# Weight loads in whole thirds, and the last half's routing with other squares, integer indices and other filler products, in a one-layer encoder with a mixture of experts

## The chip, the core and the metric

The kernel runs on one core of a Trainium2 chip. The metric is device time in microseconds (us), the median of several executions. A time with a profile is told apart from it: the profiler's execution has a span of its own (first to last instruction of the program) and a time of its own.

Engines in the rows below: PE is TensorE (PEld its weight loads), DVE VectorE, ACT ScalarE, POOL GpSimd, SP SyncE. A q behind the name (SPq) means the engine's sequencer, which issues DMAs. L599 is line 599 of the kernel.

## The reference

One encoder layer over x of 1024 tokens x 1024 features in float32: an attention branch and a gated short convolution, both projected and added to x, and then a hierarchical mixture of experts, which the change is about:

```python
h2 = rmsnorm(x, norm2_g)
g_logits = h2 @ w_rg + b_rg                      # 4 groups
grp = argmax(g_logits)                           # the best group of each token
e_in = (h2 @ w_re + b_re).reshape(t, 4, 8)[grp]  # the 8 experts of that group
top_p, top_i = top_k(softmax(e_in), 2)           # the best two of them
gates = softmax(g_logits)[grp] * top_p / sum(top_p)
out[t] = x[t] + sum over both: gate * (silu(h2 @ w_gate[e]) * (h2 @ w_up[e])) @ w_down[e]
```

There are 32 experts with an inner width of 256. The weights of one expert are 3 MB: gate and up for the first and the second half of the features, and down, three thirds of 1 MB.

## The kernel before

**Stages.** Projections and attention, then the merge of both branches in two halves of 512 tokens. For each half `out_half` computes x after the first residual, in eight column blocks of 128 (`mm`), transposes each to token rows (`turn`), writes the rows to the output and, times the norm's gain, to a table in DRAM (`h2n`), and multiplies them with the router's weights. `route` then makes the lists of the half. The routing of the first half runs beside the second half's merge; **the routing of the second half stands alone** between the merge and the experts (about 643 to 663 us of the profile).

**The last half's routing.** In `turn(7)` TensorE transposes block 7 into PSUM, ScalarE copies the block to SBUF (L850), VectorE multiplies it with the gain (L851), and `square` (L842) has ScalarE square the copied rows with a sum per token. VectorE adds the sums (L887), POOL raises the mean to the power -0.5 (L82), and VectorE scales the logits (L893). A chain of small VectorE operations follows: maximum and index per token (L904, L905), a cast of the index to float (L907), the one-hot of the group, the same for the expert (L918, L919, cast L921), and the one-hot of both experts, `ob` (L928). TensorE turns `ob` into positions (`pos`, L932 to L935), VectorE builds the matrix `A` from them (L945), and TensorE multiplies the token numbers with `A` to get the list of tokens of each expert (L952). POOL gathers the rows of experts 0 and 1 from `h2n` by that list (L1121), and TensorE transposes the gathered rows (L1132).

**Products that compute nothing.** To keep TensorE running in this stretch, `busy` (L898) issues 7 products (14 instructions) on the logits and 6 (12 instructions) on the masked expert logits, and 18 products of 512 columns follow the count (L962). Their results are not read. TensorE runs its instructions in the order in which they stand in its queue.

**The experts.** For each expert TensorE transposes the gathered rows (`px`), multiplies them with gate and up (`pgu`), ScalarE takes the silu (L1151), VectorE the product (L1153), and after two transposes (`ph`) TensorE multiplies with down (`py`). ScalarE scales the result into a buffer (L1170), and POOL adds it to the output's rows by an indirect DMA (L1173). The products run on two parts of each operand: every half third of the weights is converted to a high part (ScalarE, L1107) and a low part (VectorE, L1108), six halves for one expert. The order of ScalarE's and VectorE's work in this stage is written out by hand; `used()` says when the next half is converted.

**The stream of weights.** `load(p, s)` brings half `s` of third `p` (L599). The first 18 thirds come whole (`WHOLE`), into 16 places (12 and 13 in two halves each); places 2 and 0 are used again by thirds 16 and 17. From third 18 on every half is a DMA of its own of 512 KB into a ring of 31 half slots: those of all places except 5, whose halves hold the experts' results, and one extra tile, `more`. A load waits until its slot's last content is converted, and by a dependency written into the code for the landing of the load `DEPTH` = 4 halves before:

```python
h = 2 * p + s - DEPTH
self.tc.add_manual_dep(ins.ins, self.loads[h // 2, h % 2].ins.name, dep, reason="depth")
```

All loads go through SP's queue; half 1 of third 18 goes through POOL's, behind the two first gathers. `behind(a, b)` puts instruction a after b in the planner's order, without a wait where both are on one engine. Outside of the stage with the order by hand, a planner sets the order of each engine's queue from the dependencies and its own estimates.

## Time and profile before

| | before |
|---|---|
| median of 3 runs | 977.77 us (977.6 to 978.74) |
| the profiled execution, its own time | 980.05 us |
| its span | 977.8 us |
| PE busy / DVE / ACT / POOL | 949.3 / 736.3 / 582.7 / 115.2 us |
| mean granted clock of TensorE | 0.988 |
| DMA | 188.76 MB in 82749 packets |

The profiled execution took somewhat longer than the runs without a profile. The granted clock is a share of 2.4 GHz: 1.00 is 2.4 GHz, 0.50 is 1.2 GHz, and a value between is a stretch with both. "DMA share" is the mean busy share of the core's 16 DMA engines. The span has one stage in which TensorE, ScalarE, VectorE and the DMAs are all at work: the experts, from about 663 us to 963 us.

### The profile page before, as it was taken

Reading aid. Unit: us, or ns where it says so; the run is one execution under the profiler, and the core shown is the slowest. Engines: PE = TensorE matmul, PEld = TensorE weight load, DVE = VectorE, ACT = ScalarE, POOL = GpSimd, SP = SyncE. Lnnn points to the kernel's source line nnn. Section 1 sums busy time; section 2 is a strip of 40 time slices with the busy share of each in tenths; the row PEclk is TensorE's granted clock in tenths of the full one; section 3 lists DMA queues with packets and bytes.
Section 4 is the critical chain, followed back from the end, with each engine's and each line's share of the span. In section 5 each row is a group of like instructions: output and inputs, shape, how many; then the busy total and the mean of one; then the engine's idle time right before and its main releaser. Section 6 shows DMA issues by size and latency. Waiting matters only on the chain. (4 is left out here: it accounts for less than half of the span.)

```text
span 977.8 us, 13838 instructions
## 1 busy us (share of the span) xinstructions
PE 949.3 (97%) x4649; PEld 750.3 (77%) x4649; DVE 736.3 (75%) x1407; ACT 582.7 (60%) x1039; POOL 115.2 (12%) x90
## 2 busy tenths in 40 slices
PE   8999999999999999999999999979999999999993
PEld 5888888888878888888888888856777777777662
DVE  5777777878779656568765786478999999999882
ACT  4644555555544433346344435447999999899872
POOL 2222000000000000000000000013333232232211
PEclk9999999999999999999999999989999999999997
DMA  7201101000114233317677988768999999999993
GB/s 252 91 12 60 41 30 33 33 23 22 34 57 170 80 118 109 119 44 234 198 258 240 345 302 307 233 218 255 330 346 340 338 335 352 342 326 341 329 355 68
DMA packets 82749, 188.76 MB, mean 193 GB/s; under 512 B 10924, under 2 KB 28076, under 8 KB 80628
## 3 DMA queue, kind: packets, MB, share of 16 engines
q1 hardware_dynamic: 54772, 153.93, 45.3%
q0 software_dynamic: 7312, 17.60, 8.0%
q10 hardware_dynamic: 20592, 16.32, 5.0%
q8 instruction: 37, 0.61, 0.3%
q14 instruction: 36, 0.29, 0.1%
HBM read 166.55 MB, written 29.36 MB: 200 GB/s over the span
## 5 line engine op out<-in xcount | busy, mean ns | idle before, releaser
L1108 DVE TENSOR_TENSOR wh<-we,wh 128x1024 fp32r<-128x1024 f32 x186 | 219.8, 1217 | 29.7 <-ACT wh L1107 29.7
L1107 ACT ACTIVATE wh<-we 128x1024 fp32r<-128x1024 f32 x186 | 189.4, 1056 | 15.3 <-DMA we<-we 7.7
L70 PE MATMUL pgu<-wh,xT 128*96 128x512 f32 x768 | 190.5, 396 | 0.2 <-ACT xT L59 0.2
L70 PEld LDWEIGHTS pgu<-wh,xT 128*96 128x96 f32 x768 | 121.3, 161 | 49.9 <-ACT xT L59 0.4
L70 PE MATMUL py<-wh,hT 128*96 128x512 f32 x384 | 95.3, 395 | 3.8 <-DVE hT L60 2.0
L70 PEld LDWEIGHTS py<-wh,hT 128*96 128x96 f32 x384 | 61.4, 161 | 32.7 <-DVE hT L60 3.4
L70 PE MATMUL pc<-hT,wc_0s 128*128 128x512 f32 x288 | 77.5, 397 | 0.0
L70 PE MATMUL pc<-hT,wc_1s 128*128 128x512 f32 x288 | 75.8, 396 | 0.0
L1173 POOL DMA_INDIRECT out<-we,idx x32 | 52.6, 1644 | 183.0 <-ACT we L1170 127.4
L82 POOL TENSOR_TENSOR rstd_x<-ms_x,mhalf 128x1 f32<-128x1 f32 (+1 forms) x10 | 6.5, 651 | 573.7 <-DMA h2n<-rows 453.1
L70 PE MATMUL pq<-wq,hT 128*128 128x512 f32 (+1 forms) x384 | 71.2, 342 | 0.9 <-POOL wq L60 0.6
L70 PEld LDWEIGHTS pq<-wq,hT 128*128 128x128 f32 x384 | 59.5, 190 | 10.2 <-ACT hT L59 1.1
L70 PEld LDWEIGHTS pc<-hT,wc_1s 128*128 128x128 f32 x288 | 52.5, 188 | 9.3
L59 ACT ACTIVATE pT<-pp 128x512 fp32r<-128x512 f32 x44 | 26.1, 595 | 55.7 <-PE pp L425 55.7
L70 PEld LDWEIGHTS pc<-hT,wc_0s 128*128 128x128 f32 x288 | 52.1, 188 | 8.8 <-DVE wc_0s L60 0.3
L70 PE MATMUL po<-M,wo_1s 128*128 128x512 f32 x192 | 46.7, 391 | 0.0
L70 PE MATMUL po<-M,wo_0s 128*128 128x512 f32 x192 | 46.2, 390 | 0.0
L410 ACT ACTIVATE s<-s,nm 128x384 f32<-128x384 f32 (+1 forms) x64 | 36.9, 578 | 12.4 <-DVE nm L404 8.2
L70 PEld LDWEIGHTS po<-M,wo_1s 128*128 128x128 f32 x192 | 36.0, 188 | 8.8 <-DVE M L60 0.4
L70 PEld LDWEIGHTS po<-M,wo_0s 128*128 128x128 f32 x192 | 36.0, 188 | 7.5
L1121 POOL DMA_INDIRECT xg<-h2n,idx x32 | 35.9, 1122 | 47.7 <-PE px L1132 34.1
L1170 ACT ACTIVATE we<-py,gr 96x512 f32<-96x512 f32 x64 | 39.9, 672 | 2.4 <-PE py L70 2.4
(430 smaller groups left out, 1747.6 us busy)
## 6 DMA issues: line engine op xcount, KB each, us to landing
we<-we SPq DMA_DIRECT2D x153, 512.0 KB, 7.3
we<-we SPq DMA_DIRECT2D x16, 1024.0 KB, 7.0
sgl<-sgd SPq DMA_DIRECT2D x32, 256.0 KB, 3.6
x<-x SPq DMA_DIRECT2D x8, 512.0 KB, 4.2
wg_0r<-wcol SPq DMA_DIRECT2D x16, 256.0 KB, 2.8
wg_1r<-wcol SPq DMA_DIRECT2D x16, 256.0 KB, 2.7
wo_0r<-wo SPq DMA_DIRECT2D x16, 256.0 KB, 3.3
wo_1r<-wo SPq DMA_DIRECT2D x16, 256.0 KB, 3.6
```

What stands on the lines that cost most here:

```text
L59: a = self.nc.scalar.activation(hi, src, AF.Copy)
L70: return self.nc.tensor.matmul(*a, **k, skip_group_check=onto)
L82: self.powed = nc.gpsimd.tensor_tensor(out=r, in0=ms, in1=self.mhalf[:, :n], op=ALU.pow)
L410: ex = nc.scalar.activation(s[:, i, :nk], s[:, i, :nk], AF.Exp, bias=nm[:, i:i + 1], accum_out=sm[:, i:i + 1])
L1107: a = self.nc.scalar.activation(hl[:, 0], src, AF.Copy)
L1108: v = eng.tensor_tensor(out=hl[:, 1], in0=src, in1=hl[:, 0].bitcast(F32), op=ALU.subtract)
L1121: return self.nc.gpsimd.indirect_dma_start(out=xg[:CAP], out_offset=None, in_=self.h2n, in_offset=off, bounds_check=S, oob_is_err=False)
L1170: nc.scalar.activation(y[:C, c * 512:(c + 1) * 512], pys[c][:C], AF.Copy, scale=gate)
L1173: nc.gpsimd.indirect_dma_start(out=T["out"], out_offset=off, in_=y[:C], in_offset=None, bounds_check=S - 1, oob_is_err=False, compute_op=A ...
```

## The change

Two parts. **Stream:** thirds from 18 on come whole too, 1 MB in one DMA, except in places 12 and 13, which still take halves. The ring is the list `PLACES` of 15 places; the tile `more` is gone. A load waits for the landing of the load three thirds before. Third 18 goes whole through POOL's queue. **Routing of the last half:** block 7 is squared from PSUM, and its copy to SBUF comes behind the squares; its product with the gain is put behind the mean, and that of block 6 behind the low part of block 7; the casts L907 and L921 are gone and the integer indices are operands themselves; the `busy` products and the 18 at L962 are replaced by `fill`, products of two constants with 256 columns: 5 before block 7's transposes, 4 after its router product, 22 after the logits' transposes, 8 after the positions and 20 after the count. The position and list products are put behind the fills that stand before them.

```diff
...
 LATE = (60, 94, 94)
-WHOLE = 18
-DEPTH = 4
+DEPTH = 3
+PLACES = (2, 0, 1, 3, 4, 6, 7, 8, 9, 10, 11, 12, 13, 14, 15)
 TAP = 512
...
             r = rhs[k // 4][:, k % 4]
-            self.mm3(out, hl[:, 0, sl], hl[:, 1, sl], r[:, 0, :], r[:, 1, :], k == 0, k == n - 1)
+            last = self.mm3(out, hl[:, 0, sl], hl[:, 1, sl], r[:, 0, :], r[:, 1, :], k == 0, k == n - 1)
             if k == n // 2 - 1 and mid is not None:
                 mid()
+        return last
...
-        whole = p not in (12, 13) and p < WHOLE
+        whole = self.place(p) not in (12, 13)
         if (p, s) in self.loads:
...
         elif p >= 16 and whole:
-            self.raw[p] = self.raw[(2, 0)[p - 16]]
+            self.raw[p] = self.raw[self.place(p)]
         j = self.order[p]
         to, sl = (self.raw[p], slice(0, 2048)) if whole else (self.half_of(p, s), slice(s * 1024, (s + 1) * 1024))
-        q = self.nc.gpsimd if (p, s) == (18, 1) else self.nc.sync
+        q = self.nc.gpsimd if p == 18 else self.nc.sync
         ins = q.dma_start(to, self.T["we"][j // 3, j % 3, :, sl])
...
             self.behind(ins, self.wrote)
-        if (p, s) == (18, 1):
+        if p == 18:
             self.behind(ins, self.gathered)
...
             dep = mybir.DependencyInfo(mybir.DependencyClass.Sync, mybir.DependencyReason.DATA)
-            h = 2 * p + s - DEPTH
-            self.tc.add_manual_dep(ins.ins, self.loads[h // 2, h % 2].ins.name, dep, reason="depth")
+            self.tc.add_manual_dep(ins.ins, self.loads[p - DEPTH, s].ins.name, dep, reason="depth")
+
+    def place(self, p):
+
+        return p if p < 16 else PLACES[(p - 16) % len(PLACES)]
...
+        p = self.place(p)
         if p in (12, 13):
             return self.raw[p, s]
-        if p < 16:
-            return self.raw[p][:, s * 1024:(s + 1) * 1024]
-        return self.slots[(2 * p + s - 32) % len(self.slots)]
+        return self.raw[p][:, s * 1024:(s + 1) * 1024]
...
             po = ps.tile([P, 512], F32, name=f"po_{half}_{i}", tag=("pg", "pp")[i % 2], bufs=2)
-            self.proj(po, wg, half, rhs=self.M, mid=(lambda: turn(i - 1)) if i > 0 else None)
+            self.proved = self.proj(po, wg, half, rhs=self.M, mid=(lambda: turn(i - 1)) if i > 0 else None)
             self.added = nc.vector.tensor_add(x2, po, x2)
             self.x2s = [self.sgp.tile([P, 512], F32R, name=f"x2s_{half}_{i}_{b}", tag="sg", bufs=2) for b in range(2)]
-            self.split(x2, *self.x2s)
-
-        def square(i):
+            self.xlow = self.split(x2, *self.x2s)[1]
+            if i == 7 and half == 1:
+                self.fill(5, self.proved, None)
+
+        def square(i, pt=None):
             for t in range(4):
-                if i < 6:
+                if pt is not None:
+                    sq, R = self.sq[:, t % 2 * P:(t % 2 + 1) * P], pt[:, t]
+                elif i < 6:
                     sq, R = self.sq[:, 0:2 * P].rearrange("p (b c) -> p b c", b=2), self.rows[:, :, 0, t]
...
             R, hg = self.rows[:, i % 2, 0], self.rows[:, i % 2, 1]
-            nc.scalar.activation(R, pt, AF.Copy)
+            fast = i == 7 and half == 1
+            if fast:
+                square(7, pt)
+            copied = nc.scalar.activation(R, pt, AF.Copy)
+            if fast:
+                self.behind(copied, self.squared)
+                self.squared = copied
             self.gained.append(nc.vector.tensor_tensor(out=hg, in0=pt, op=ALU.mult,
...
             for b in range(2):
-                nc.tensor.matmul(pl, self.wrt[:, i].rearrange("p a c -> p (a c)"), self.x2s[b],
-                                 start=(i == 0 and b == 0), stop=(i == 7 and b == 1))
-            if i % 2 == 1 or i == 6:
+                m = nc.tensor.matmul(pl, self.wrt[:, i].rearrange("p a c -> p (a c)"), self.x2s[b],
+                                     start=(i == 0 and b == 0), stop=(i == 7 and b == 1))
+            if fast:
+                self.fill(4, m, None)
+            elif i % 2 == 1 or i == 6:
                 square(i)
...
         for i in range(8):
+            if i == 7:
+                self.idle = ps.tile([P, 512], F32, name=f"idle_{half}", tag="pg", bufs=2)
             mm(i)
...
         for t in range(4):
-            nc.tensor.matmul(plt[:, t], lT[:, t * P:(t + 1) * P], self.twice[:2 * NW], start=True, stop=True)
+            m = nc.tensor.matmul(plt[:, t], lT[:, t * P:(t + 1) * P], self.twice[:2 * NW], start=True, stop=True)
+        if half == 1:
+            m = self.fill(22, m, None)
         s1 = new([4], "s1")
...
         r = self.rstd(rp, s1, 4, D, "x2")
+        if half == 1:
+            self.behind(self.gained[7], self.meant)
         if half == 1:
...
-        def busy(x, n):
-            for i in range(n if half == 1 else 0):
-                nc.tensor.matmul(self.pl[:, 0:x.shape[1]], self.ident[:, 0:2 * NW], x, start=True, stop=True)
-
-        busy(lt.rearrange("p t c -> p (t c)"), 7)
         gl, el = lt[:, :, 0:NG], lt[:, :, 8:8 + NE].rearrange("p t (g j) -> p t g j", g=NG)
...
             nc.vector.max_index(gi[:, t], gm[:, t], lt[:, t, 0:8])
-        gf = new([4], "gf")
-        nc.vector.tensor_copy(gf, gi[:, :, 0])
+        gf = gi[:, :, 0]
         og = new([4, NG], "og")
...
         nc.vector.tensor_tensor(out=es, in0=el, in1=bc(og[:, :, :, None], [P, 4, NG, NJ]), op=ALU.mult)
-        busy(work[:, 256:384], 6)
         ei = new([4, NJ], "ei")
...
         ec = new([4, 2], "ec")
-        nc.vector.tensor_copy(ec, ii[:, :, 0:2])
-        nc.vector.scalar_tensor_tensor(ec, bc(gf[:, :, None], [P, 4, 2]), float(NJ), ec, op0=ALU.mult, op1=ALU.add)
+        nc.vector.scalar_tensor_tensor(ec, bc(gf[:, :, None], [P, 4, 2]), float(NJ), ii[:, :, 0:2], op0=ALU.mult,
+                                       op1=ALU.add)
         O = self.O[:, :, ts, :]
...
         pf = pp.rearrange("p t e -> p (t e)")
-        nc.tensor.matmul(pf, self.uob[:, 0, :], ob.rearrange("p t e -> p (t e)"), start=True, stop=False)
+        first = nc.tensor.matmul(pf, self.uob[:, 0, :], ob.rearrange("p t e -> p (t e)"), start=True, stop=False)
+        if half == 1:
+            self.behind(first, m)
         for t in range(3):
             nc.tensor.matmul(pp[:, t + 1:4], self.uob[:, 1, :], bc(ob[:, t:t + 1], [P, 3 - t, NE]), start=False, stop=False)
-        nc.tensor.matmul(pp, self.uob[:, 1, :], bc(self.osum[:, None, :], [P, 4, NE]), start=False, stop=True)
+        m = nc.tensor.matmul(pp, self.uob[:, 1, :], bc(self.osum[:, None, :], [P, 4, NE]), start=False, stop=True)
+        if half == 1:
+            m = self.fill(8, m, None)
         bi = new([4, 4, NE], "bg", F32R)[:, 0:2]
...
             for t in range(4):
-                nc.tensor.matmul(pI, A[:, c, t], bi[:, c, t], start=(c + t == 0), stop=(c + t == 4))
+                x = nc.tensor.matmul(pI, A[:, c, t], bi[:, c, t], start=(c + t == 0), stop=(c + t == 4))
+                if half == 1 and c + t == 0:
+                    self.behind(x, m)
         if half == 0:
...
             counted = nc.tensor.matmul(pn, self.uob[:, 1, :], self.osum, start=True, stop=True)
-            for i in range(18):
-                warm = nc.tensor.matmul(self.pl, self.uob[:, 1, 0:2 * NW],
-                                      self.O.rearrange("p a t e -> p (a t e)"), start=True, stop=True)
-                self.behind(warm, counted)
+            self.fill(20, counted, None)
             mx = new([1], "mx")
...
+    def fill(self, n, at, to):
+
+        for i in range(n):
+            m = self.nc.tensor.matmul(self.idle[:, 0:2 * P], self.uob[:, 1, :], self.uob.rearrange("p a b -> p (a b)"),
+                                      start=True, stop=True)
+            self.behind(m, at)
+            at = m
+        return at
+
     def half(self, p, s):
...
             self.behind(self.added, v)
-            self.behind(self.gained[6], self.added)
+            self.behind(self.gained[6], self.xlow)
...
         run = [self.expert(e, lambda c, s, e=e: self.w[3 * e + c, s], self.used, xgs[e % 2], xts[e % 2],
-                           lambda e=e: self.slots[0] if e == NE - 1 else self.half_of(5, e % 2),
+                           lambda e=e: self.half_of(2, 0) if e == NE - 1 else self.half_of(5, e % 2),
                            self.idx[:CAP, 1, e:e + 1], self.gr[:CAP, 0, e:e + 1], self.gr[:CAP, 1, e:e + 1])
...
             self.gathered = self.gather(xgs[e], self.idx0[:CAP, e:e + 1])
-        order = [(p, s) for p in [2, 0, 1] + list(range(3, 16)) for s in range(2)]
-        self.slots = [self.half_of(*h) for h in order if h[0] != 5]
-        self.slots.insert(4, self.sp6.tile([P, 1024], F32, name="more"))
         for p in range(17, 19):
...
```

## Rows read from the trace of the kernel before

**Rows 1.** Busy time by stretch: us, busy (instructions) by engine, clock, DMA share, GB/s
```profile
692.00:907.00 215.00, 215.00 (x1083) 155.01 (x1082) 198.23 (x235) 199.82 (x281) 65.13 (x48) 1.00 1.03 341
907.00:957.00 50.00, 47.10 (x226) 32.41 (x225) 40.66 (x48) 40.12 (x58) 10.83 (x7) 1.00 1.00 335
```
**Rows 2.** ScalarE in order of time: start, us, instruction [idle before <-releaser]
```profile
898.03 0.47 ACT L1151 ACTIVATE sg<-pgu,gr 96x256 f32<-96x256 f32 x1 [0.35 <-PE pgu L70]
...
907.20 0.47 ACT L1151 ACTIVATE sg<-pgu,gr 96x256 f32<-96x256 f32 x1 [0.34 <-PE pgu L70]
...
909.44 1.06 ACT L1107 ACTIVATE wh<-we 128x1024 fp32r<-128x1024 f32 x1 [0.82 <-DMA we<-we]
...
949.25 0.48 ACT L1151 ACTIVATE sg<-pgu,gr 96x256 f32<-96x256 f32 x1
...
956.61 0.47 ACT L1151 ACTIVATE sg<-pgu,gr 96x256 f32<-96x256 f32 x1 [0.56 <-PE pgu L70]
```
**Rows 3.** Waits from 860 to 966 us: who for whom, total, times, longest
```profile
ACT wh L1107 <- DMA we<-we: 7.7, 7, 1.9
```
**Rows 4.** TensorE in order of time, one expert's transposes
```profile
683.33 0.82 PE L1132 MATMUL px<-ident,xg 96*128 96x96 f32 x8
```
**Rows 5.** DMA queues, 692 to 907 us: packets, MB, share of 16 engines
```profile
q1 hardware_dynamic: 16763, 61.03, 78.5%
q0 software_dynamic: 5244, 12.12, 24.3%
```
**Rows 6.** Instructions of L1107 by stretch: us, busy (count), clock, DMA share, GB/s
```profile
692.00:907.00 215.00, 141.22 (x140) 1.00 1.03 341
```
**Rows 7.** All engines in order of time, the last half's routing
```profile
643.54 0.60 ACT L850 ACTIVATE rows<-pt 128x512 f32<-128x512 f32 x1 [0.43 <-PE pt L848]
...
644.17 0.31 ACT L842 ACTIVATE sq<-rows 128x128 bf16<-128x128 f32 x1
...
644.99 0.68 DVE L851 TENSOR_TENSOR rows<-pt,g 128x512 f32<-128x512 f32 x1
...
645.13 1.08 PE L885 MATMUL plt<-twice,work 80*128 80x40 f32 x8 [0.78 <-DVE work L882]
...
649.21 0.17 DVE L907 CAST gf<-gi 128x4 f32<-128x4 uint32 x1
...
651.95 2.36 PE L898 MATMUL pl<-work,ident 128*80 128x128 f32 x12
652.38 0.22 DVE L928 TENSOR_TENSOR ob<-O 128x128 bf16<-128x128 bf16 x1
...
654.15 0.22 PE L932 MATMUL pos<-ob,uob 128*128 128x128 bf16 x1
...
654.56 0.48 DVE L940 TENSOR_TENSOR work<-O,pos 128x128 f32<-128x128 bf16 x2 [1.63 <-PE pos L935]
...
657.58 5.54 PE L962 MATMUL pl<-O,uob 128*80 128x512 bf16 x18
...
662.84 0.76 PEld L1132 LDWEIGHTS px<-ident,xg 96*128 96x128 f32 x8 [0.19 <-DMA xg<-h2n,idx]
```
**Rows 8.** PE by stretch: us, busy (count), granted clock, DMA share, GB/s
```profile
646.00:648.00 2.00, 0.21 (x2) 0.73 0.98 377
...
652.00:654.00 2.00, 2.00 (x12) 0.56 1.05 430
...
656.00:658.00 2.00, 1.33 (x10) 0.79 0.03 8
658.00:660.00 2.00, 2.00 (x6) 0.50 0.00 0
660.00:662.00 2.00, 2.00 (x9) 0.85 0.79 209
```
**Rows 9.** DMA queues, 692 to 697 us, halves of weights alone: all packets
```profile
DMA packets 543, 1.97 MB, mean 393 GB/s; under 512 B 63, under 2 KB 63, under 8 KB 543
```
**Rows 10.** DMA queues, 651 to 655 us, whole thirds of weights alone: all packets
```profile
DMA packets 223, 1.68 MB, mean 420 GB/s; under 512 B 18, under 2 KB 18, under 8 KB 18
```

## The prediction

> **What bounds the kernel now.** I read the busy shares by stretch first. From 692 to 907 us TensorE has work in every microsecond, and the DMA engines are as full, while VectorE and ScalarE keep some 7% free [rows 1]. So in the long stretch of the experts two resources are at their limit at once, and the question is which of them ends an expert. ScalarE's order of time tells it. The silu of one expert (L1151) follows that of the one before by 9.17 us, from 898.03 to 907.20, and waits for TensorE's product [rows 2]: up to there TensorE sets the pace. From 909.44 on the conversions of the weights (L1107) wait for DMA [rows 2]. The table of waits has seven such waits, 7.7 us in all [rows 3].
>
> What that costs is read from the silus. Between 907.20 and 949.25 lie four experts and 42.05 us, where 4 x 9.17 makes 36.68: 5.4 us too many. The next interval is 7.36 us where 8.35 were due, as the last expert has no successor whose eight transposes (0.82 us [rows 4]) come in between; so 1.0 comes back. **4.4 us are lost to late weights**, all of it after 907.
>
> Why weights come late is a matter of counting. In the 215 us from 692 to 907 the queue of the weights moved 61.03 MB [rows 5], 116.4 halves of 524,288 bytes, and ScalarE converted 140 [rows 6]. The ring of buffers gave up 23.6 halves of lead and was empty two microseconds later, when the first wait comes. In the 45 us that are left, to the last conversions at about 952 on an undisturbed pace, another 45 x 23.6/215 = 4.9 halves are missing. They cost 4.4 us, 0.90 us each.
>
> The second place is the last half's routing, 643 to 663 us: a chain of small VectorE operations with two visits to TensorE, which ends when the first gathered rows arrive and the transposes of expert 0 begin, at 662.84 [rows 7]. Nothing hides it. What delays expert 0 delays all 32, as TensorE is full afterwards.
>
> **The routing, step by step.** *Squares from PSUM.* Now the copy L850 starts at 643.54 and the squares at 644.17 [rows 7]. Reading the transposes in place, the squares start where the copy does: 0.63 us gained. They are the same four instructions; that PSUM is slower to read than SBUF is not seen (the copy takes 0.60 for 512 columns). The copy then runs beside the mean and the power that follow, and so does the product with the gain (two of L851 at 0.68 each, of which the change ties the last behind the mean [rows 7]); without that cover it would cost its 0.68 in front of the logits. Its write to h2n leaves SP some 0.7 us later, and so do the loads queued behind it on SP, the last ones to be converted of all that is loaded by then. The product of column block 6 ends later too, and ScalarE's queue, which issues its write, must wait for it. If the planner puts that issue in front of the squares they lose the 0.63 again; I take 0, as nothing early reads that write.
>
> *Two casts fall away*, L907 and its like L921: 2 x 0.17 = 0.34 us of a VectorE chain without gaps [rows 7]. The operations that now read integers have the same shapes; a slower reading of integers is bounded by the casts themselves, so 0 to 0.34, and I take 0.34.
>
> *TensorE's dummy products.* Today 12 products of L898 run from 651.95 for 2.36 us. The one-hot sum `ob` is ready at 652.38 + 0.22 = 652.60, but the position product L932 stands behind them and starts at 654.15, and VectorE sits idle for 1.63 us before L940 [rows 7]. The new fills hang on no data of the chain: 22 go off after the logits' transposes (L885, over at 646.21), 8 after the positions, 20 after the counts. What a fill lasts is bounded by L962, 18 products of 512 columns in 5.54 us [rows 7], of which some 3.1 are at half clock [rows 8]: (3.1 + 2 x 2.4)/18 = 0.44 us for one at half clock, 0.22 for 256 columns. So 22 take at most 4.8 us and are over at about 651.1, just before `ob`, now due at 651.6. The 1.55 us between 652.60 and 654.15 shrink to a hand-over of some 0.15: 1.40 gained. Against that, TensorE may have been idle before the positions and run them at 1.2 GHz. From 654.15 to 654.56 their chain takes 0.41 us; doubled, it costs up to 0.4. I take 0.3. Sum: 0.63 + 0.34 + 1.40 - 0.3 = **2.1 us**, between 1.0 (squares and casts bring nothing, positions at half clock) and 2.4.
>
> **The stream.** Whole thirds instead of halves, three in flight instead of four halves, 15 places instead of 31 half slots; places 12 and 13 still take halves. What one byte costs is read from stretches in which one kind runs alone: halves (4 KB packets) 393 GB/s [rows 9], whole thirds (8 KB packets) 420 GB/s [rows 10]. So 512 KB takes 1.334 or 1.248 us, and with 13 of 15 places whole a half saves 0.0745. In the experts' stretch the weights' queue holds 78.5% of the engines' time [rows 5], 215 x 0.785/116.4 = 1.450 us per half; less the saving, 1.3755. If gathers and scatters (24.3%) keep their time, 215 us bring 122.7 halves, and the deficit falls from 23.6 to 17.3.
>
> The lead shrinks too. The ring has 30 halves for 31; a place is free only when both its halves are converted, and a half is usable only when its whole has landed: half a unit to one each. I take 2.5, so 21.1 are left of 23.6. From 692 to 952 the deficit eats 260 x 17.3/215 = 20.9 of them: just enough. That is too close to call free, and I leave one half missing, 0.9 us. Of 4.4 us **3.5 come back**. With no saving at all 260 x 23.6/215 = 28.5 are wanted and 7.4 missing: 6.7 us lost, 2.3 more than today. With half the saving (119.5) 3.7 are missing, 3.3 us, a gain of 1.1. The deeper queue gives nothing by itself, as the engines are full [rows 1].
>
> The Trainium skill (DMA: Bandwidth & Descriptors, Measured) sets 1 MiB as the size from which a DMA reaches at least 75% of the peak, and lets far more be expected of the doubled size; by it no half would be missing and the sum would be 2.1 + 4.4 = 6.5 us. Rows 9 and 10 speak against so large a step: with several loads in flight the two sizes differ by 6.9%.
>
> Whole load 18 goes through POOL's queue and now waits for both halves of place 1. Behind it stands the gather for expert 2, which cannot start before expert 0's transposes anyway: 0.
>
> **Sum.** 2.1 + 3.5 = 5.6 us. The profiled execution took 980.05 us (span 977.8), 2.3 over the median of 977.77. Against its own time that is 974.4; carried to the median, **972.2 us**.
>
> **Rivals.** *A, the forecast:* both parts work, 970 to 974. Chance 0.47.
>
> *B, a cold start.* The last fills are 20 x 256 columns where 18 x 512 stand now, which kept TensorE busy until the gather came. At half clock 20 last 4.4 us, at full clock half of that, and up to 2 us more are then empty before the transposes. What an empty TensorE brings here stands in rows 8: the clock falls within 646 to 648, with 0.21 of 2 us busy, and again within 656 to 658, and each time stays at 1.2 GHz under full load for a while, some 6.8 and 3.4 us by the shares. If the experts start so, half of that is lost, 1.7 to 3.4: 973.9 to 975.6. For it: nothing fills the gap. Against: the fills may end late enough. Chance 0.24. The Trainium skill (TensorE: Matmul & The Clock Gate, The HAM clock gate) has it that the slow state is the default and activity releases it; rows 8 agree.
>
> *C, the saving is lost in the mix:* beside gathers and scatters a longer packet may be stalled in proportion. Half or none of the saving: 974.6 to 978.0. Against: rows 5 give the weights 61.03 MB at 78.5%, 362 GB/s of engine time, not far under the 393 of rows 9, so most of a packet's time is the same as alone. Chance 0.19.
>
> *D, slower:* the weights' stream gets slower, because scatters stall longer packets for longer and loads land in lumps of 1 MB. The place is the ring after 900 us. At an unchanged rate the ring's loss (2.3) outweighs the routing's gain (2.1); each 1% below that loses 1.2 of 116.4 halves, 1.4 over 260 us, 1.3 us. At 2% less the time is 980.6. Against: rows 10. Chance 0.07.
>
> *E, the change doesn't do what it says:* the planner sets ScalarE's write in front of the squares, or a fill in front of the positions. 0.6 to 1.4 us less gained: 972.8 to 973.6. Chance 0.03.
>
> **How the numbers follow.** A measurement of this kernel tells 0.2%, 2 us, from no change. Faster by more: A, B but for 0.04 at its far end, the upper half of C, E: 0.81. Within: 0.12, from the ends of B and C. Slower: 0.07, D. The range runs from 970.0 (all of 4.4 and 2.4 back is 971.0, and 1 us for what the median may hold beyond the profiled run) to 977.0, which leaves out D and the end of C.
>
> **What would show it.** The waits of L1107 for DMA should nearly vanish, the silus keep 9.17 us to the end, the weights' queue carry more than 61.03 MB in 215 us. The positions should follow `ob` within 0.2 us and expert 0's transposes start near 660.8. I am wrong if waits for DMA stay or start before 900, or if the granted clock is 0.5 while the first products of the experts run.

## The result and the profile after

The changed kernel takes **983.67 us** (median of 6 runs, 981.13 to 988.56) against 977.89 for the kernel before (6 runs beside it): ratio 1.006, 95% interval 1.0039 to 1.0081. It is 0.6% slower, and the interval does not hold 1, where 972.2 us and a range up to 977.0 were forecast. The profiled execution took 981.48 us, span 979.1, and is one of the quicker ones; a second profiled execution took 983.62.

First what came as foretold. The routing of the last half, answering to [rows 7], in TensorE's order of time (start, us, instruction, idle before it):

```profile
645.52 2.58 PE L1109 MATMUL idle<-uob 128*128 128x256 bf16 x22
650.81 0.23 PE L946 MATMUL pos<-ob,uob 128*128 128x128 bf16 x1 [2.72 <-DVE ob L942]
...
652.91 1.43 PE L970 MATMUL pI<-bg,A 128*96 128x32 f32 x8 [0.84 <-DVE A L963]
...
654.79 4.43 PE L1109 MATMUL idle<-uob 128*128 128x256 bf16 x20
660.35 0.85 PE L1158 MATMUL px<-ident,xg 96*128 96x96 f32 x8 [1.13 <-DMA xg<-h2n,idx]
```

The positions now wait for `ob` (L942, started at 650.53, 0.23 long) and not for dummy products. Expert 0's transposes start at 660.35, 19.12 us after the start of the projection's last sum (L831, 641.23); before it was 21.20 (641.76 to 662.96). That is 2.1 us, as forecast. Nor does any conversion of weights (L1133) wait for a load behind 692 us, and the queues, answering to [rows 5], show that the stream carries more (692 to 907 us: packets, MB, share of the 16 engines; then the scatters, the indirect DMAs that add an expert's result to the output, with their number and their median from issue to landing):

```profile
q1 hardware_dynamic: 10009, 64.48, 80.2%
q0 software_dynamic: 4928, 11.43, 21.8%
...
out<-we,idx POOLq DMA_INDIRECT x22, 8.9
```

The weights' queue carries 64.48 MB, 123.0 halves; 122.7 were forecast. Most of its bytes now come in packets of 8 KB; places 12 and 13 still take 4 KB.

The last line holds what went wrong. In the kernel before the same line, over the same stretch, reads:

```profile
out<-we,idx POOLq DMA_INDIRECT x24, 7.8
```

So a scatter of an expert's result takes 1.1 us longer at the median. Busy time by stretch, to be held against [rows 1]:

```profile
692.00:907.00 215.00, 211.26 (x1050) 151.16 (x1049) 193.46 (x227) 194.80 (x273) 70.69 (x45) 1.00 1.02 354
907.00:957.00 50.00, 48.24 (x238) 34.30 (x236) 41.87 (x51) 42.11 (x60) 14.46 (x10) 1.00 0.82 262
```

TensorE, which had work in all 215 us before, has 3.7 us without, and 33 instructions fewer in the same stretch; the DMAs fall to 0.82 after 907, where they were at 1.00: the stream is done early and something else is late. The waits for DMA from 660 to 966 us say what (who for whom: us, times, longest):

```profile
POOL out L1199 <- DMA out<-we,idx: 9.8, 2, 5.8
ACT we L1196 <- DMA out<-we,idx: 6.8, 10, 1.5
PE px L1158 <- DMA xg<-h2n,idx: 6.6, 11, 1.2
```

ScalarE's copy of a result (L1196) waits ten times for the scatter that still reads the buffer it wants to fill; TensorE's transposes wait eleven times for gathered rows, whose gather stands behind a scatter in GpSimd's queue. The first line is at the end of the program, and a wait of 5.9 us like it was there before too. Before, neither of the other two stood in the table but for one wait of 0.2 us; the late weights of [rows 3] did. ScalarE's order of time shows the first such wait and its growth:

```profile
730.19 0.47 ACT L1177 ACTIVATE sg<-pgu,gr 96x256 f32<-96x256 f32 x1 [0.34 <-PE pgu L70]
739.36 0.47 ACT L1177 ACTIVATE sg<-pgu,gr 96x256 f32<-96x256 f32 x1 [0.33 <-PE pgu L70]
...
825.29 1.26 ACT L1196 ACTIVATE we<-py,gr 96x512 f32<-96x512 f32 x2 [0.22 <-DMA out<-we,idx]
832.04 0.47 ACT L1177 ACTIVATE sg<-pgu,gr 96x256 f32<-96x256 f32 x1 [0.33 <-PE pgu L70]
835.98 1.26 ACT L1196 ACTIVATE we<-py,gr 96x512 f32<-96x512 f32 x2 [1.49 <-DMA out<-we,idx]
842.63 0.47 ACT L1177 ACTIVATE sg<-pgu,gr 96x256 f32<-96x256 f32 x1 [1.30 <-PE pgu L70]
```

The silus keep 9.17 us (730.19 to 739.36), and from about 820 they come later, at worst 10.59 us apart (832.04 to 842.63).

**The chain.** Each scatter adds into `out`, so each waits for the landing of the one before, and starts 0.8 us after it at the earliest. Call a scatter *chained* if it starts just so. Pairing each start with the landing before it, 27 of the 29 pairs whose landing the trace of the kernel after has are chained; before, 14 of 31. One link is a scatter and 0.8. Before, that was a mean of 7.7 + 0.8 = 8.5 us (experts 5 to 25) against TensorE's 9.17: the chain had time to spare and caught up. Now it is 9.1 + 0.8 = 9.9, and the scatters of experts 5 to 26 go off every 9.91 us. They fall back by some 0.7 per expert; the two result buffers cover that with one period of slack, 9.2 us. By the trace a scatter starts 0.3 us behind the end of its rows' copy at expert 3 and 9.1 us behind it at expert 14; the copy for expert 16, at 825.29 above, is the first that waits for its buffer, and from there the chain sets the pace. From the first silu to the last (669.77 to 957.83, for 672.43 to 956.61) it takes 288.1 us instead of 284.2. With nothing in the way it takes 280.0 (below), so **4.2 us lost to late weights became 8.1 lost to late scatters**. The own times of the profiled executions add up: earlier first silu -2.7, longer experts +3.9, together +1.2; measured are +1.4 (981.48 to 980.05). This accounts for that pair alone: a second pair of profiles (r12 and r11 below) is 4.0 us apart, and the medians 5.8. Both profiled executions of the kernel before lie some 2 us above its median, and the first of the kernel after 2 us below its own.

### The profile page after: what moved, and what is told of

It is laid out like the page before. It is cut to its first block, busy times and chain, and to the rows that moved or that the text cites. A ratio compares the mean times of both kernels' runs of the same rounds, so it can differ in the third digit from the quotient of the medians.

```text
span 979.1 us, 13599 instructions
## 1 busy us (share of the span) xinstructions
PE 947.3 (97%) x4664; PEld 748.4 (76%) x4664; DVE 736.5 (75%) x1403; ACT 581.9 (59%) x1039; POOL 126.6 (13%) x90
## 5 line engine op out<-in xcount | busy, mean ns | idle before, releaser
L1134 DVE TENSOR_TENSOR wh<-we,wh 128x1024 fp32r<-128x1024 f32 x192 | 226.3, 1218 | 31.4 <-ACT wh L1133 31.1
L1133 ACT ACTIVATE wh<-we 128x1024 fp32r<-128x1024 f32 x192 | 194.2, 1054 | 7.6 <-DVE ob L942 4.8
L1147 POOL DMA_INDIRECT xg<-h2n,idx x32 | 46.1, 1441 | 33.5 <-PE px L1158 17.3
L1196 ACT ACTIVATE we<-py,gr 96x512 f32<-96x512 f32 x64 | 40.1, 674 | 9.6 <-DMA out<-we,idx 6.8
```

The costliest lines, as they stand in the source:

```text
L1133: a = self.nc.scalar.activation(hl[:, 0], src, AF.Copy)
L1134: v = eng.tensor_tensor(out=hl[:, 1], in0=src, in1=hl[:, 0].bitcast(F32), op=ALU.subtract)
L1147: return self.nc.gpsimd.indirect_dma_start(out=xg[:CAP], out_offset=None, in_=self.h2n, in_offset=off, bounds_check=S, oob_is_err=False)
L1196: nc.scalar.activation(y[:C, c * 512:(c + 1) * 512], pys[c][:C], AF.Copy, scale=gate)
```

## The experiments

Two theories. *Packets*: the 8 KB packets of the weights lengthen the scatters (*P*). *Bytes in flight*: it is the 3 MB in flight instead of 2 (*F*). Beside them, what each half of the change does alone. The expectations call the account above, with its chain and P, theory T. "Scatter" below is the mean of experts 5 to 25 from issue to landing (some traces lack some landings; then it is of those that they have), "silus" the time from the first silu to the last, MB that of the weights' queue from 700 to 900 us.

**r1_routing**: the kernel after with the stream of before; `load`, `half_of` and the list of 31 half slots as there.

```diff
-DEPTH = 3
-PLACES = (2, 0, 1, 3, 4, 6, 7, 8, 9, 10, 11, 12, 13, 14, 15)
+WHOLE = 18
+DEPTH = 4
```

> The routing of the change with the stream of before (halves, four in flight, 31 slots). Theory T (the routing works, the loss is the scatters' chain, which longer packets slow down): the experts start 2 to 2.5 us earlier, scatters land after about 8 us as before, weights still come late by 4 us at the end; ratio to before 0.9975 to 0.998, some 975.5 to 976. Rival C (the loss is in the routing or in a colder start of the experts): over 980.

Measured: 977.59 us, ratio 1.0014 [0.9995, 1.0033]; scatter 7.5. The conversions still wait for late weights, 3.1 us in four waits. From last sum to transposes 18.98 us: the gain is there, but the median has none of it, so the 975.5 to 976 expected did not come. Two things in the profile may have eaten it. TensorE's products run slower in this execution, 995 instructions in 200 us

```profile
700.00:900.00 200.00, 200.00 (x995) 142.99 (x994) 182.82 (x216) 184.04 (x258) 54.93 (x44) 1.00 1.02 337
```

where before it were 1006 at the same granted clock of 1.00, and the first half's routing has a new wait of 1.1 us. More on both below.

**r2_stream**: the other half alone, the kernel before with these lines (and `load`, `place`, `half_of` and the last expert's buffer) of the kernel after.

```diff
-WHOLE = 18
-DEPTH = 4
+DEPTH = 3
+PLACES = (2, 0, 1, 3, 4, 6, 7, 8, 9, 10, 11, 12, 13, 14, 15)
```

> The whole thirds with the routing of before. Theory T: scatters land after about 9 us, one waits for the one before it, and with the 0.8 us between a landing and the next issue they come every 10 us, over the 9.17 us of an expert; no conversion waits for weights; ScalarE waits for the result buffer from the 13th expert on; 2 us above the changed kernel, some 985 to 986, ratio 1.008. Rival C: about 978 or less.

Measured: 985.79, ratio 1.0093 [1.007, 1.0115]; scatter 9.2, 27 of 29 chained, silus 289.8, no late weights but for one wait of 0.5 us. The whole loss is in the stream.

**r3_pairs**: the kernel after, each third from 19 on in two loads of 512 KB, six in flight. The same places and the same 3 MB, in 4 KB packets.

```diff
-        whole = self.place(p) not in (12, 13)
+        whole = self.place(p) not in (12, 13) and p < 19
...
-        elif p >= 16 and whole:
+        elif p >= 16 and self.place(p) not in (12, 13):
```

> The changed kernel, but every third from 19 on comes as two loads of 512 KB with 4 KB packets, in the same places, with the same 3 MB in flight. Theory P (the scatter loses its turns to longer packets): scatters land after about 8 us and ScalarE does not wait for result buffers; the weights move at the old rate and come late again, 4 to 7 us; 975 to 979. Rival F (it is the 3 MB in flight instead of 2 that the scatters queue behind): scatters still take about 9 us, 983 or more.

Measured: 977.18, ratio 0.9994 [0.998, 1.0009]; scatter 7.8, 6 of the 21 pairs with a landing chained, no copy waits, no late weights, 59.46 MB (before 56.51). With the same bytes in flight the smaller loads and packets alone take the loss away: that speaks for P, and F alone cannot be it. The rate was not the old one, though, and the weights were not late again, as was expected: with 4 KB packets the stream carries nearly what whole thirds carry (59.95), so its gain comes from the deeper queue.

**r4_two**: the kernel after with 2 MB in flight in 8 KB packets.

```diff
-DEPTH = 3
+DEPTH = 2
```

> The changed kernel with two whole thirds in flight instead of three, 2 MB as in the kernel before, 8 KB packets. Theory P: scatters still take about 9 us and their chain still sets the pace; within 2 us of the changed kernel, 982 to 985. Rival F: scatters back at about 8 us, no waits for result buffers, 974 or less.

Measured: 992.36, ratio 1.0153 [1.0091, 1.0216]; 54.76 MB, and weights late as never before:

```profile
ACT wh L1133 <- DMA we<-we: 19.8, 10, 3.0
```

Scatter 7.0, though the silus keep 9.2 us until expert 22. Neither theory had this: P expected 9 us here, F some 974 us in all. So long packets do not hurt by themselves; with two of them in flight the weights' queue holds 75.1% of the engines' time instead of 80.1. By these runs it takes both, long packets and three of them in flight.

**r5_deep**: the kernel before with one number changed.

```diff
-DEPTH = 4
+DEPTH = 6
```

> The kernel before with one number changed: six halves of 512 KB in flight instead of four (3 MB as the change has, but in 4 KB packets; the old routing). If the rate of the stream comes from the bytes in flight and not from the packets' size, ScalarE's conversions wait for no late weights behind the first experts (140 conversions waited 4.4 us in all before), the scatters take about 7.8 us, and the time is 4.4 us less than before: about 973. If what the prediction held is right (the engines are full and a deeper queue gives nothing), the late weights stay and the time is 977. If the experts' products start 236 ns apart, as in r1_routing and r3_pairs, instead of 232 ns, then 36 of them in each of some 28 experts give back up to 3 us: 975 to 977 without late weights. The 232 or 236 also tells whether the slower products belong to the new routing's start of the experts (232 here) or to a queue that never stalls them (236 here).

Measured: 976.66, ratio 1.0001 [0.9981, 1.0021]. In the profile what was foretold for the deeper queue: 59.63 MB, no late weights, silus 280.0 us, span 972.6. But the scatter takes 8.4 us where 7.8 were expected, and 28 of 29 are chained: a link is 9.16 against 9.17, just enough. So the deeper queue lengthens scatters too, with 4 KB packets as well. The medians are 1.8 us apart, of 4.2, and the interval holds a ratio of 1.

**r6_both**: r1_routing with the same edit of `DEPTH`.

> The new routing with the stream of before (halves, all slots) and six halves in flight. Against r5_deep it is the routing alone, with no late weights to hide it: 2.0 us less, if the routing's gain reaches the end (about 971 if the products start 232 ns apart, 974 if 236). If the products start 236 ns apart here and 232 in r5_deep, the routing's gain is eaten by them, and the two are within 1 us. If r6_both beats both kernels of the case by over 0.2%, it is what the change should have been.

Measured: 976.72, ratio 0.999 [0.9965, 1.0015]; scatter 7.8, no late weights: within 0.1 us of r5_deep, as was expected if the products run at the slower pace, which they do in its profile (silus 283.4). In the profiled execution (980.37) the experts start cold, at a granted clock of 0.50:

```profile
666.00:668.00 2.00, 2.00 (x8) 1.54 (x8) 0.75 (x2) 1.06 (x1) 0.00 (x0) 0.50 0.13 37
```

and first transposes to first silu take 12.1 us instead of 9.4.

**r7_short**: the kernel after, scattering only 32 of an expert's 96 rows (`y[:32]` goes with it); the result lacks the others.

```diff
-        off = bass.IndirectOffsetOnAxis(ap=idx, axis=0)
+        off = bass.IndirectOffsetOnAxis(ap=idx[:32], axis=0)
```

> The kernel after, with each expert's sums scattered for its first 32 rows only, so 64 of 96 rows are left out of the result; everything else, the load of 1 MB and its 8 KB packets too, stays. If the chain of scatters (each waits for the landing of the one before it, 9.1 us and 0.8 us, against 9.17 us of an expert's products) is what holds the kernel after, a scatter then takes 4 to 7 us, no copy of an expert's result waits for a scatter, no expert takes over 9.4 us, and the time falls from 983.7 to 970 to 974. If whole thirds slow the experts in another way (converting from the ring, GpSimd's gathers, slower products), the time stays above 979.

Measured: 975.70, ratio 0.997 [0.9951, 0.9989]. From the scatter's own rows:

```profile
DMA to landing us min/median/max: 3.5/6.3/6.7
```

No copy waits, and every scatter but the last starts 0.3 us behind the copy of its rows, so none is chained (the trace has the landings of seven). 8 us of the kernel after are gone. The stream, which now shares with less, even carries 64.60 MB. The time is above the 970 to 974 expected; in the profile the products run at the slow pace here too (silus 283.4).

**r8_three**: the kernel after with a third result buffer.

```diff
+        more = self.sp6.tile([P, 1024], F32, name="more")
...
-                           lambda e=e: self.half_of(2, 0) if e == NE - 1 else self.half_of(5, e % 2),
+                           lambda e=e: self.half_of(2, 0) if e == NE - 1 else more if e % 3 == 2 else self.half_of(5, e % 3),
```

> The kernel after, with three buffers for an expert's result instead of two (the third is the tile that the kernel before had as an extra slot). If the chain of scatters is the bound, a third buffer only moves where the waiting is done: ScalarE's copies wait later, but the last scatter starts no sooner, 27 or so scatters stay chained, and the time is within 2 us of 983.7. If the two buffers are the bound (a result waits for the scatter two experts back, while the scatters themselves could go faster), no copy waits any more and the time falls by the 5 to 7 us of these waits, to 977 to 979 or less.

Measured: 983.63, ratio 1.0059 [1.0035, 1.0082]. The copies wait no more; what waits is the next thing in GpSimd's queue behind a scatter that cannot start, the gather of the expert after next:

```profile
PE px L1158 <- DMA xg<-h2n,idx: 4.7, 7, 1.5
```

27 of 30 chained, silus 289.3. The chain is the bound and not the buffers.

**r9_warm**: r6_both with more constant products.

```diff
-            m = self.fill(8, m, None)
+            m = self.fill(12, m, None)
...
-            self.fill(20, counted, None)
+            self.fill(27, counted, None)
```

> r6_both with more of the constant products: 12 instead of 8 behind the positions and 27 instead of 20 behind the count, so that TensorE does not stand for 0.84 us ahead of the list products and for 1.03 us ahead of the first expert's transposes, as it did in r6_both, whose granted clock then stayed at 0.50 until 668 us (first transposes to first silu 12.1 us, against 9.4 us in r1_routing and in the kernel before). If those idle stretches caused the cold start, the granted clock is 1.00 from 664 us on, transposes to silu take 9.4 us, and the time is up to 2.7 us below r6_both's profiled run, 971 to 974 with products 232 ns apart and 974 to 976 with 235.5. If the cold start has another cause, transposes to silu take 10 us or more here too, and the time stays where r6_both is, 976.7; the additional products can also hold the first transposes up by some 0.5 us.

Measured: 978.15, ratio 1.0003 [0.9986, 1.002]. The profiled execution is what was hoped for: clock 1.00 from 646 to 674 us, 9.4 us to the first silu, silus 280.1, 973.66 us. The median is 4.5 above it. So the profile of one execution does not stand for the kernel.

**r10_oldpairs**: r2_stream with the two edits of r3_pairs.

> The kernel before with the stream of r3_pairs (thirds by place, six halves in flight) and the old routing: against r3_pairs it is the routing alone undone, against r5_deep only the places differ. If the slower pace of the experts' products (235.5 ns instead of 232) belongs to the new routing, they start 232 ns apart here as in the three old-routing profiles so far, no weight is late, and the time is within 2 us of r5_deep: 974 to 977. If it is a pace that any kernel falls into when nothing stalls the products, 235.5 ns shows here too, at 977 to 979. Scatters take 7.8 to 8.4 us with either, as the packets are 4 KB.

Measured: 976.31, ratio 0.9993 [0.9981, 1.0004]; products at 232 ns, silus 280.0, scatter 8.4. Against r2_stream (9.2) the size alone is changed once more. And this one trace has both kinds of scatter: up to expert 9 they start at most 0.7 us behind the copy of their rows and take 7.7 us on average; from expert 12 to 27 all are chained, as far as the landings are in the trace, and take 8.4. So with one size of packet and one depth the late ones are the longer ones; which of the two brings the other is not shown.

**r11_before_again, r12_after_again**: both kernels unchanged, for a second profile.

> The kernel before once more, unchanged, for a second profiled execution: r5_deep and r10_oldpairs have no late weights, and their profiled spans are 4 to 5 us shorter than the profiled span of before (977.8), but their medians are only 1 to 2 us below. If the 4.4 us of late weights belong to every execution of before, this one shows 3.5 to 5 us of waits of ScalarE's conversions behind 800 us, with products 232 ns apart. If they were more than usual in the one profiled execution, this one shows under 3 us of them, and the span is 974 to 976.

> The kernel after once more, unchanged, for a second profiled execution. By the chain of scatters: 25 or more scatters start 0.8 us behind the landing of the one before, a scatter takes 9.0 to 9.3 us on average, ScalarE's copies of a result or the transposes behind them wait 5 us or more in all from about 815 us on, and no conversion of the experts' weights waits for a load. A cold start of the experts (first transposes to first silu over 10.5 us instead of 9.4) comes in some executions of the new routing (3 of 8 profiled so far); if it comes here, the span is 2 to 3 us above the 979.1 of the first profile.

Measured: 979.63 and 983.62. Before: conversions late by 9.7 us in 10 waits from 902 on, silus 284.7, scatter 7.5. After: 28 of 31 chained, scatter 9.2, ScalarE's copies wait 7.7 us in 9 waits, silus 289.4, no late weights, no cold start. Both readings repeat.

**r13_first, r14_first_again**: here something else had to be explained, which the traces of all new-routing kernels show. From the last sum of the *first* half to the first sum of the second they take 53.6 to 54.5 us; with the old routing it is 53.4 in all five profiles. In r1_routing TensorE's waits from 560 to 597 us hold one line where before there is none:

```profile
PE pG L1027 <- DVE bg L1023: 1.1, 1, 1.1
```

The two casts fall away in the first half too, and a tile for the fills (`idle`) is made there that nothing uses. There the routing runs beside projections and the planner weaves its products in; in r1_routing the gates' products (pG) then stand ahead of where VectorE has their operands. r13_first is r9_warm with both undone in the first half, the casts left in and the tile not made:

```diff
-            if i == 7:
+            if i == 7 and half == 1:
...
+        if half == 0:
+            gf = new([4], "gf")
+            nc.vector.tensor_copy(gf, gi[:, :, 0])
...
+        io = ii[:, :, 0:2]
+        if half == 0:
+            nc.vector.tensor_copy(ec, io)
+            io = ec
```

> r9_warm with the two casts left in the first half's routing and the idle tile made in the last half alone, so that TensorE's order in the first half is that of the kernel before. If the wait ahead of the first half's gate products comes from that order, the stretch from the last sum of the first half to the first sum of the second is 53.4 us again (54.3 in r9_warm, 53.6 to 54.5 in the others with the new routing), the last sum lies at 641 to 642, expert 0's transposes at 659.5 to 660.7, and the median is 0.9 us below r9_warm's 978.2 as far as a median can tell; with the granted clock at 1.00 and products 232 ns apart the span is 969.5 to 971.5. If the stretch stays above 53.6, the lost time between the halves has another cause. If the median stays above 976 although the profile shows all of this, the rest is in what differs between executions (the products' pace, the start).

> The same kernel as r13_first for a second profiled execution. The stretch between the halves (53.4) and from the last sum to the transposes (18.6 to 19.2) should repeat within 0.3 us, as they are set by the order of the work. The pace of the experts' products may differ: if it is 232 ns in one and 235.5 ns in the other execution of one kernel, the pace belongs to the execution and not to the change, and costs 3 us between the first and the last silu (280.0 against 283.4).

Measured: the stretch is 53.4 in both profiles, as in the kernel before, and the wait is gone, so it was the change's own. Whether the casts or the tile made it, these runs do not tell. From the last sum to the transposes it is 19.2 and 18.6 us; these were to agree within 0.3. Median 976.15, ratio 0.9981 [0.9961, 1.0002], the lowest beside r7_short, and not told from before; the single execution of r14 took 978.22. Both profiles have a half-cold start (10.8 and 10.6 us to the first silu) and slow products (silus 283.4). r13_first carries 59.95 MB from 700 to 900, as much as the kernel after does, in 4 KB packets, with scatters of 7.7 us against 9.1.

## Why the prediction was wrong

*The stream's rate* was right (122.7 halves forecast, 123.0 measured), for a wrong reason. "The deeper queue gives nothing by itself, as the engines are full" does not stand: with 4 KB packets and six in flight r5_deep carries 59.63 MB, whole thirds 59.95, two wholes in flight 54.76. A half then holds 1.40 us of the engines' time in r5_deep as in the kernel after (200 us x share / halves), where before it was 1.45: the saving is there without any longer packet, and nothing shows that the size brings more. A DMA share of 1.03 did not mean that no more could be carried. That no weights would be late came true (the sum left one half missing); that the halves came to the forecast number was luck.

*The step that failed* is "if gathers and scatters (24.3%) keep their time", and with it the sum, which has no term for what waits for a single scatter. As a share of the engines they kept it, and the share even fell (24.3 to 21.8%); from issue to landing they did not: scatters went from 7.7 to 9.1 us. The chain of scatters had 9.17 - 8.5 = 0.7 us to spare per expert, a resource near its limit that the tables of waits of the kernel before do not show, since with slack nobody waited for it. The price by the chain is (9.9 - 9.17) x some 26 links, 19 us, less the 9.2 us of slack in the buffers: some 10; the silus show 8.1 and 9.4 over 280.0. r3_pairs (shorter packets) and r7_short (shorter scatters) each take it away, and r8_three (more buffers) does not.

Where the 1.4 us come from is shown only in part. From 700 to 900 us the weights' packets last 348 ns on average at 8 KB and 180 at 4 KB before, while the 4 KB packets of the gathers and scatters last no longer than before (262 ns, 273 before). So it may be the turns in between that grew. A scatter has 96 rows; on 16 engines that would be six packets each, and if each waits for one packet of the other queue, six times 0.17 make 1.0 us, an estimate from these rows. The Trainium skill (DMA: Bandwidth & Descriptors, Queues, rings and completion order) says that each engine takes turns between the queues, a packet at a time. The 7.8 us of r3_pairs and the 9.1 of the kernel after agree with that. The estimate is not the whole account: r4_two has the same packets and 7.0 us, r5_deep has 4 KB packets and 8.4, and by r10_oldpairs a chained scatter takes 0.7 us more than one in time. In every run here, besides, the size of a load changes together with that of its packets. How the 1.4 us divide between size, depth and being late is open.

*Rival D* had the sign with 0.07, but the mechanism the other way round: it let scatters stall the weights, and the ring after 900 decide. What happened is that the stream of weights slows the scatters, which fall behind from expert 4 on, and that the experts feel it from 820 on.

*The routing* came to 2.1 us as forecast, and 18.6 to 19.2 us in eleven profiles against 20.9 to 21.2 in five. By the times of both traces, each from its last sum, the logits are 0.92 us earlier (0.63 was forecast for the squares), the casts give 0.40 (0.34) and the hand-over to the positions 1.49 (1.40). Two things take back 0.7 where 0.3 was put: the gather lands 0.2 us later, and the list products take 1.43 us where they took 0.89, as here (before, then the clock after: us, busy, granted clock, DMA share, GB/s):

```profile
656.24 0.89 PE L952 MATMUL pI<-bg,A 128*96 128x32 f32 x8 [1.71 <-DVE A L945]
...
654.00:656.00 2.00, 1.57 (x10) 0.50 0.38 160
```

The 22 fills were not over at 651.1, just before `ob`, but at 648.1: they ran at a clock of 1.00 and took 2.58 us and not up to 4.8. TensorE then stood for 2.72 us, and the granted clock fell between 652 and 656; the cold products are the list's and not the positions'. So the sum is right in part by errors that cancel. What was missed is that the same code runs for the first half, where 0.3 to 1.1 us are lost again. The change was costed at one place and made at two.

*Rival B*, the cold start, did not come in either profile of the kernel after (9.4 us to the first silu), but it exists: r4_two, r6_both, r8_three, r13_first and r14_first_again, 5 of the 11 profiles with the new routing, take 1.2 to 2.7 us longer from the first transposes to the first silu; none of the five with the old routing does. r9_warm, with the gaps filled, started warm; r13_first, with the same fills, did not, so filling them is not shown to be a remedy.

*What stays open.* Without late weights and with short scatters the profiles promise some 4 us, and medians give 0 to 2. Whether the late weights cost 4 us in executions without a profile is not shown. One part is the pace of the experts' products: most start 232 to 233 ns apart or 235 to 236, at the same granted clock of 1.00, and the slower pace makes the silus 283.4 us instead of 280.0. All five profiles with the old routing begin at the quicker pace, seven of the eleven with the new one run at the slower through the first 100 us. Where experts stall it changes, and either way: r8_three began slow and goes back and forth from 850 us on, and r2_stream, with the old routing, began quick and runs slow from 890 on. It does not hang on VectorE working beside (median 236 ns with it and without it in r1_routing); ScalarE is at work in nearly all of them. What sets it was not found, and the timed runs have no trace that would tell how often it comes.

## What to carry to other kernels

Before a change to a stream, list the chains in which each transfer waits for the landing of the one before, and hold one link against the period of the bound; a chain with 8% to spare appeared in no table of waits here, and was the next bound. Larger packets were not free for the transfers on the other queue: depth in 4 KB packets gave the same bytes with scatters of 7.8 to 8.4 us instead of 9.1. And an edit in code that runs twice is costed at both places, above all where a planner sets the order of the engines.

## What the runs showed that was not expected

The 340 GB/s of a DMA share of 1.03 rose to 355 GB/s by nothing but two more loads of 512 KB in flight (r5_deep, 700 to 900 us). A single scatter of 96 rows of 4 KB takes 4.6 us at the end, when the weights are through, 7.7 in r13_first beside 4 KB packets and 9.1 in the kernel after beside 8 KB packets at the same 59.95 MB. TensorE showed two paces for the same products at one granted clock, 232 and 236 ns by the median, each kept for long stretches.
